# ScalarE in place of GpSimd for half of a 16-bit split ahead of a transposing DMA

## The chip, the cores and the metric

The kernel runs on 1 core of one Trainium2 chip. The metric is device time in microseconds, as a median of runs. Engine names follow the profile: PE is TensorE (matmul), PEld its weight loads, DVE VectorE, ACT ScalarE, POOL GpSimd, SP SyncE, which here only issues DMAs.

## What is computed

Two layers of a hybrid block over 256 tokens and 16 meta tokens (272 columns; the kernel keeps only the 258 it still needs towards the end of the second layer), width 1024. Each layer projects the normed input into retention, HGRN2 and differential attention, joins the three branches through gates, and ends in a convolutional feed-forward part. The change lies in differential attention, 8 heads per layer, each with two softmaxes:

```python
s = jnp.einsum('bqhmd,bkhmd->bhmqk', qb, k)
p = jax.nn.softmax(jnp.where(allowed, s, MASK_VALUE), axis=-1)
w = p[:, :, 0] - lam * p[:, :, 1]
return jnp.einsum('bhqk,bkhe->bqhe', w, v)
```

The weights `w` come out with queries on the partitions. The last product needs keys there, so `w` has to be transposed.

## The kernel before

**Main work.** Nearly all of PE's time goes to products of weights streamed from HBM, in 404 chunks of 8 tiles of 128x128. For each chunk, a DMA on SP's queue brings `wraw` (3 buffers), ACT copies it to `whi` (the rounded part), DVE subtracts to get `wlo` (the rest), each with 4 buffers. PE then makes three matmuls a tile: L943, L944 and L945. Chunk numbers stand in the names: `whi115` is the rounded half of chunk 115.

**Attention beside it.** `da_heads` (L1412 on) does two heads at a time: 2 layers x 2 groups x 2 pairs, so 8 pairs and 16 heads. PE makes the scores `ds`, DVE the masked maximum, ACT the exponentials, DVE the two scalings that leave `w` in the tile `two_a`. The second softmax's tile, `two_b`, is then free, and takes the 32-bit words of `w` parted into their upper and lower 16-bit halves, 3 blocks of 128 queries-by-keys words. A head does this in two instructions: ACT parts one block (L1463, 128x2x128 values), POOL the two others (L1464, 128x2x256 values). ACT also copies the block's short tail into `dt`. `turn` issues a DMA on SP's queue that transposes `two_b` back into `two_a`'s memory, and ACT copies the result, put together into words again, to `wts`. PE multiplies `wts` with the values `vt` into `do`, in one of two PSUM banks that accumulate (`acc_bank`). ACT copies two short pieces (`dot`) out of `do` and DVE the rest (`da`), and only then is the bank free for a later head. `da_tail` deals with a group's tails at once: `wt` is a transposition of `dt` on PE, DVE makes `tw` of it, and PE another `do` from `tw` and `vs`.

**Order.** The kernel is not written in the order in which it runs. Each operation goes into a plan with an estimated cost, and a list scheduler (`plan.issue`) writes the order of all engines and of SP's queue by these costs, the due times of the weights and the buffers that are free. A 16-bit copy that reads SBUF costs the planner 0.094 us + 1.163 ns a column on ACT, and 0.34 us + 0.85 ns a column on POOL. Once written, an engine's order is fixed: an instruction that waits holds up all behind it on its engine or queue. Since helpers record nearly every operation, the profile gives most instructions the line L634, and names tell them apart.

Of the kernel before, what the change touches and what calls it, by code (L numbers as in the profile page):

```python
# [15 lines left out]
AF = mybir.ActivationFunctionType  # L16
# [4 lines left out]
P = 128  # L21
# [671 lines left out]
def _trace(ctx, tc, plan, a, depth, probe):  # L693
    nc = tc.nc
    act = _Engine(plan, nc.scalar, "act", 0.094, 0.833e-3)
    dve = _Engine(plan, nc.vector, "dve", 0.068, 1.042e-3)
    pe = _Engine(plan, nc.tensor, "pe", 0.0, 4 / 2400)
    pool = _Engine(plan, nc.gpsimd, "pool", 0.04, 0.85e-3)
# [30 lines left out]
    def temp(cols, tag, bufs=2):  # L729
        return new(tp, [P, cols], F32, tag, bufs, tag)  # L730
# [7 lines left out]
    def acc_bank(name):  # L738
        return new(bp, [P, 512], F32, "acc", 2, name)

    def tt(out, x, y, op):
        dve.tensor_tensor(out=out, in0=x, in1=y, op=op)

    def stt(out, x, s, y, op0, op1):
        dve.scalar_tensor_tensor(out=out, in0=x, scalar=s, in1=y, op0=op0, op1=op1)

    def ts(out, x, s1, s2, op0, op1=ALU.bypass):
        dve.tensor_scalar(out=out, in0=x, scalar1=s1, scalar2=s2, op0=op0, op1=op1)
# [230 lines left out]
    def words(t):  # L979

        return t.bitcast(U16).rearrange("p (t h) -> p h t", h=2)

    def turn(to, src):

        turned = to.rearrange("p (n x) -> p n x", x=P)
        sync.dma_start_transpose(turned, src)
        return turned.rearrange("p (h n) x -> p h n x", h=2)
# [54 lines left out]
    for li in range(depth):  # L1042
# [370 lines left out]
        def da_heads(b, heads):  # L1413

            q, k, vt, out = st[f"dq{b}"], st[f"dk{b}"], st[f"dvt{b}"], st[f"da{b}"]
            scale = DA_DH ** -0.5

            a1s = [temp(T + P + TAIL, "wts") for _ in heads]
            tiles = ((META + P, T, 0), (META, META + P, T))
            sbs = [[temp(2 * T, tag) for tag in ("two_a", "two_b")] for _ in heads]  # L1420
            sss = [[new_bank("ds") for _ in range(2)] for new_bank in (bank, acc_bank)]
            stats = []
            for _ in heads:
                red = temp(12, "dm")
                stats.append([red[:, 4 * i : 4 * i + 4].rearrange("p (t m) -> p t m", m=2) for i in range(3)])


            def scores():
                for ss, hd in zip(sss, heads):
                    for q0, nk, at in tiles:  # L1430
                        for m in range(2):
                            half = slice(64 * m, 64 * m + 64)
                            nc.tensor.matmul(ss[m][:, at : at + nk], q[half, hd, q0 : q0 + P], k[half, hd, :nk], start=True, stop=True)  # L1433

            got = plan.add("pe", scores, 1.8, [x[:, : T + P + META] for ss in sss for x in ss], [q[:, heads[0] : heads[-1] + 1, :], k[:, heads[0] : heads[-1] + 1, :]], count=32)
            plan.hold(*sum(sbs, []), *a1s)
            for a1, hd in zip(a1s, heads):
                pool.tensor_copy(a1[:, :META], st[f"dw{b}"][:, hd * META : (hd + 1) * META])
                plan.queue(plan.ops[-1], got)
            for ss, sb, (nm, _, _) in zip(sss, sbs, stats):  # L1440
                for i, (q0, nk, at) in enumerate(tiles):
                    mask = const[:, C_MASK + T - nk : C_MASK + T]
                    for m in range(2):
                        cols = slice(at, at + nk)
                        dve.tensor_tensor_reduce(out=sb[m][:, cols], in0=ss[m][:, cols], in1=mask, scale=1.0,
                                                 scalar=-3e38, op0=ADD, op1=ALU.max, accum_out=nm[:, i, m : m + 1])
                ts(nm, nm, -scale, None, MUL)
            for sb, (nm, sm, cf) in zip(sbs, stats):
                for i, (q0, nk, at) in enumerate(tiles):
                    for m in range(2):  # L1450
                        p = sb[m][:, at : at + nk]
                        act.activation(p, p, AF.Exp, bias=nm[:, i, m : m + 1], scale=scale, accum_out=sm[:, i, m : m + 1])
                dve.reciprocal(cf, sm)
                tt(cf[:, :, 1], cf[:, :, 1], nlam[:, li : li + 1].to_broadcast([P, 2]), MUL)
                for i, (q0, nk, at) in enumerate(tiles):
                    p0, p1 = (x[:, at : at + nk] for x in sb)
                    ts(p1, p1, cf[:, i, 1:2], None, MUL)
                    stt(p0, p0, cf[:, i, 0:1], p1, MUL, ADD)
            for a1, sb, hd in zip(a1s, sbs, heads):
                w = sb[0]  # L1460
                src, to = (x[:, : 3 * P].bitcast(U16) for x in (sb[1], w))
                parts = src.rearrange("p (h t) -> p h t", h=2)
                act.activation(parts[:, :, :P], words(w[:, T : T + P]), AF.Copy)  # L1463
                pool.tensor_copy(parts[:, :, P:], words(w[:, : 2 * P]))  # L1464
                act.activation(st[f"dt{b}"][:, :, hd, :], tails_of(w), AF.Copy)
                turned = turn(to, src)
                act.activation(words(a1[:, META : META + 3 * P]), turned.rearrange("p h n x -> p h (n x)"), AF.Copy)
            for a1, hd in zip(a1s, heads):
                o = acc_bank("do")
                ec = slice(hd * P, hd * P + P)  # L1470
                pe.matmul(o[:, t0:T], vt[:, 0, ec], a1[:, t0:T], start=True, stop=False)
                pe.matmul(o[:, P + META : T], vt[:, 1, ec], a1[:, T : T + P], start=False, stop=True)
                for g, c in ((0, 2 * P), (1, P)):
                    act.activation(st[f"do{b}"][:, g, hd, :], o[:, c : c + TAIL], AF.Copy)
                dve.tensor_copy(out[:, hd, t0 : 2 * P], o[:, t0 : 2 * P])
                sub_norm(out[:, hd, t0 : 2 * P], out[:, hd, t0 : 2 * P])

        def tails_of(w):

            return bass.AP(w.tensor, w.offset + 2 * P, [list(w.ap[0]), [T - P, 2], [1, TAIL]])  # L1480

        def sub_norm(out, o):
            n = o.shape[1]
            r = temp(T, "hr")[:, :n]
            head_rsqrt(r, o, AF.Square)
            stt(out, o, subg[:, li : li + 1], r, MUL, MUL)
# [123 lines left out]
        for name, j in ORDER:  # L1610
            if name == "+ret":
                behind(ret_tail, "ret", 2)
                for hd in range(RET_HEADS):
                    behind(lambda: ret_head(hd), "ret", 2)
            elif name in ("+hga", "+hgb"):
                b = "ab".index(name[3])
                st[f"hgo{b}"] = behind(lambda: hg_heads(b), "hg" + name[3])
            elif name in ("+hgoa", "+hgob"):
                behind(st["hgo" + str("ab".index(name[4]))], "hgo" + name[4])
            elif name in ("+daa", "+dab"):  # L1620
                b = "ab".index(name[3])
                st[f"da{b}"] = slot4("da")
                behind(lambda: da_first(b), "da", 2)
                for hd in (0, 2):
                    behind(lambda: da_heads(b, (hd, hd + 1)), "da", 2)
                behind(lambda: da_tail(b), "da", 2)
            elif name[0] == "!":
                settle(name[1:])
            elif name[0] == "*":
                plan.key = clock[0] - MARGIN  # L1630
                n = name[1:]
                if n == "b2":
                    blocks = [st["da0"], st["da1"]]
                else:
                    t = st["rg" if n == "b0" else "hg"]
                    blocks = [t[:, 0:4, :], t[:, 4:8, :]]
                st["x" + n] = split_blocks(n, blocks, t0)
# [88 lines left out]
            elif name == "fi":  # L1726
# [16 lines left out]
                for f in range(2):  # L1743
                    ft = j + f * FK
                    w = lambda i: small[:, S_CW + (li * 3 + i) * 2 * FK + ft : S_CW + (li * 3 + i) * 2 * FK + ft + 1]
# [49 lines left out]
```

## Time and profile before

| | |
|---|---|
| median of 3 runs | 1279.19 us (1279.06 to 1281.21) |
| the profiled execution | 1278.5 us |
| its span in the trace | 1276.1 us |
| PE busy | 1267.3 us |
| DVE busy | 961.8 us |
| ACT busy | 871.5 us, 1481 instructions |
| POOL busy | 140.5 us, 125 instructions |

Busy time is the union of an engine's instructions in the trace. Some 2.4 us of the profiled execution lie around the span. The weights' stream feeds PE all the time, and the heads' chains run beside it on the other engines, so that a long busy time on these engines costs nothing by itself: time is lost where PE has nothing it may do next.

### The profile page before, as it was taken

How to read it: one execution, taken by the hardware profiler on the slowest of the kernel's cores; microseconds unless marked ns; L12 is line 12 of the kernel's file. 1: busy time of each engine (PE TensorE's matmuls, PEld its weight loads, DVE VectorE, ACT ScalarE, POOL GpSimd, SP SyncE). 2: the span in 40 equal slices, each digit the busy share in tenths (PEclk: the TensorE clock that was granted, in tenths of full speed). 3: DMA queues.
4: the chain of work that ended last, by engine and by line, in shares of the span. 5: the costliest groups of instructions: out<-in, count | busy, mean ns of one | idle time of the engine just before them, and what ended most of it. 6: DMA issues, size and time to landing. Idle time of an engine off the chain costs nothing.

```text
span 1276.1 us, 26835 instructions
## 1 busy us (share of the span) xinstructions
PE 1267.3 (99%) x10760; PEld 1246.5 (98%) x10760; DVE 961.8 (75%) x1690; ACT 871.5 (68%) x1481; POOL 140.5 (11%) x125
## 2 busy tenths in 40 slices
PE   9999999999999999999999999999999999999998
PEld 9999999999999999999999999999999999999986
DVE  8585887698785789886575858886987867998753
ACT  7776485857786577776456654858577865788743
POOL 1001101312232000000000011012232210000000
PEclk9999999999999999999999999999999999999999
DMA  7764685646656655556555656856556666677663
GB/s 235 246 184 133 191 219 139 164 150 166 190 154 187 189 173 179 172 178 182 173 177 180 182 166 176 219 152 166 157 154 199 183 197 187 181 197 205 202 191 106
DMA packets 102059, 229.19 MB, mean 180 GB/s; under 512 B 48176, under 2 KB 48304, under 8 KB 101936
## 3 DMA queue, kind: packets, MB, share of 16 engines
q1 hardware_dynamic: 101648, 226.97, 61.4%
q8 instruction: 84, 1.38, 0.4%
q10 hardware_dynamic: 288, 0.52, 0.1%
q14 instruction: 39, 0.32, 0.1%
HBM read 216.19 MB, written 1.05 MB: 170 GB/s over the span
## 4 chain that ended last, share of the span: by engine, by line
PE 95%; issue 2%; DVE 1%; POOL 1%; ACT 0%; DMA 0%; SPq 0%; ACTq 0%; POOLq 0%; DVEq 0%
PE main L945 29%; PE main L943 28%; PE main L944 28%; PE fo L1586 1%; PE fo L1584 1%; PE fo L1585 1%; PE ds L1433 1%; PE ro L634 1%; POOL hr L634 1%; PE do L634 1%; PE ho L1016 1%; PE lev L1152 1%; PE s L634 0%; PE px L1016 0%; PE far L1152 0%
## 5 line engine op out<-in xcount | busy, mean ns | idle before, releaser
L943 PE MATMUL main<-xh,whi 128*128 128x272 f32 (+1 forms) x2368 | 682.0, 288 | 0.1
L945 PE MATMUL main<-xh,wlo 128*128 128x272 f32 (+1 forms) x2368 | 679.8, 287 | 0.2 <-DVE wlo L634 0.2
L944 PE MATMUL main<-xl,whi 128*128 128x272 f32 (+1 forms) x2368 | 670.2, 283 | 0.0
L634 DVE TENSOR_TENSOR wlo<-wraw,whi 128x1024 fp32r<-128x1024 f32 (+1 forms) x408 | 499.4, 1228 | 217.3 <-ACT whi L634 215.8
L634 ACT ACTIVATE whi<-wraw 128x1024 fp32r<-128x1024 f32 (+1 forms) x408 | 426.8, 1048 | 185.3 <-PE main L944 124.3
L944 PEld LDWEIGHTS main<-xl,whi 128*128 128x128 f32 x2368 | 449.4, 190 | 0.0
L943 PEld LDWEIGHTS main<-xh,whi 128*128 128x128 f32 x2368 | 445.5, 188 | 1.2 <-ACT whi L634 0.4
L945 PEld LDWEIGHTS main<-xh,wlo 128*128 128x128 f32 x2368 | 444.5, 188 | 0.7 <-DVE wlo L634 0.6
L634 POOL PARTITION_ALL_REDUCE hr<-hsq x36 | 74.3, 2091 | 174.4 <-ACT hsq L634 159.0
L634 DVE SCALAR_TENSOR_TENSOR two_b<-u,small,two_b 128x256 f32<-128x256 f32 (+2 forms) x176 | 78.7, 492 | 0.2
L945 PE MATMUL main<-ghi,wlo 128*128 128x272 f32 x176 | 51.1, 290 | 0.0
L943 PE MATMUL main<-ghi,whi 128*128 128x272 f32 x176 | 50.8, 288 | 0.0
L944 PE MATMUL main<-glo,whi 128*128 128x272 f32 x176 | 50.2, 285 | 0.0
L634 ACT ACTIVATE two_b<-u,small 128x272 f32<-128x272 f32 (+1 forms) x88 | 49.1, 598 | 1.1 <-DVE glo L634 1.0
L634 POOL PARTITION_ALL_REDUCE rstd<-sum x4 | 10.5, 2614 | 326.5 <-PE main L944 193.5
L634 ACT ACTIVATE u<-main 128x544 f32<-128x544 f32 (+1 forms) x40 | 24.4, 610 | 28.2 <-PE main L945 28.1
L943 PE MATMUL main<-b0hi,whi 128*128 128x272 f32 (+1 forms) x128 | 37.4, 292 | 0.0
L943 PE MATMUL main<-b1hi,whi 128*128 128x272 f32 (+1 forms) x128 | 36.9, 288 | 0.0
L945 PE MATMUL main<-yhi,wlo 128*128 128x272 f32 (+1 forms) x128 | 36.5, 285 | 0.0
L945 PE MATMUL main<-b2hi,wlo 128*128 128x272 f32 (+1 forms) x128 | 36.5, 285 | 0.0
L945 PE MATMUL main<-b1hi,wlo 128*128 128x272 f32 (+1 forms) x128 | 36.5, 285 | 0.0
L945 PE MATMUL main<-b0hi,wlo 128*128 128x272 f32 (+1 forms) x128 | 36.5, 285 | 0.0
(256 smaller groups left out, 1940.8 us busy)
## 6 DMA issues: line engine op xcount, KB each, us to landing
wraw<-in_w SPq DMA_DIRECT2D x402, 512.0 KB, 3.7
h<-in_h SPq DMA_DIRECT2D x4, 272.0 KB, 4.8
dec<-in_dec SPq DMA_DIRECT2D x2, 544.0 KB, 5.4
wraw<-in_w SPq DMA_DIRECT2D x4, 256.0 KB, 4.4
const<-in_const SPq DMA_DIRECT2D x1, 937.0 KB, 8.4
gain<-in_gl SPq DMA_DIRECT2D x1, 512.0 KB, 4.5
out<-y ACTq DMA_DIRECT2D x2, 256.0 KB, 2.7
out<-y SPq DMA_DIRECT2D x2, 256.0 KB, 2.7
```

Of the source, the lines that this page charges most:

```text
L634: self.plan.add(self.name, lambda: f(*args, **kw), cost, outs, ins, self._kind(method, args, ins), count)
L943: nc.tensor.matmul(o, wh, hi, start=first, stop=False)
L944: nc.tensor.matmul(o, wh, lo, start=False, stop=False)
L945: nc.tensor.matmul(o, wl, hi, start=False, stop=last)
L1016: nc.tensor.matmul(o, x, y, start=first, stop=last)
L1152: nc.tensor.matmul(o, keys, x, start=True, stop=True)
L1433: nc.tensor.matmul(ss[m][:, at : at + nk], q[half, hd, q0 : q0 + P], k[half, hd, :nk], start=True, stop=True)
L1584: nc.tensor.matmul(o, gh, wh, start=first, stop=False)
L1585: nc.tensor.matmul(o, gl, wh, start=False, stop=False)
L1586: nc.tensor.matmul(o, gh, wl, start=False, stop=end)
```

## The change

One line: the two blocks that POOL parted are parted by ACT. The values written and where they go are the same.

```diff
@@ -1461,7 +1461,7 @@
                 src, to = (x[:, : 3 * P].bitcast(U16) for x in (sb[1], w))
                 parts = src.rearrange("p (h t) -> p h t", h=2)
                 act.activation(parts[:, :, :P], words(w[:, T : T + P]), AF.Copy)
-                pool.tensor_copy(parts[:, :, P:], words(w[:, : 2 * P]))
+                act.activation(parts[:, :, P:], words(w[:, : 2 * P]), AF.Copy)
                 act.activation(st[f"dt{b}"][:, :, hd, :], tails_of(w), AF.Copy)
                 turned = turn(to, src)
                 act.activation(words(a1[:, META : META + 3 * P]), turned.rearrange("p h n x -> p h (n x)"), AF.Copy)
```

It runs once per head, 16 times. The planner sees other costs and another engine, and so writes another order around each pair. POOL's other instructions keep their order.

The first place is the last pair of layer 1, whose heads have `two_a_337` and `two_a_339`. ACT's rows there before the change:

```order
L634 ACTIVATE whi114_800<-wraw114_799 128x4x256
L634 ACTIVATE two_b_340_691<-two_a_339_690 128x2x128
L634 ACTIVATE dt_315_666<-two_a_339_690 128x2x16
L634 ACTIVATE whi115_803<-wraw115_802 128x4x256
L634 ACTIVATE wts_335_686<-two_a_337_688 128x2x384
L634 ACTIVATE wts_336_687<-two_a_339_690 128x2x384
L634 ACTIVATE whi116_807<-wraw116_806 128x4x256
L634 ACTIVATE dot_316_667<-do_347_698 128x16
L634 ACTIVATE hsq_349_700<-da_310_661 128x256
L634 ACTIVATE dot_316_667<-do_347_698 128x16
L634 ACTIVATE m2_380_797<-main_379_790 128x544
L634 ACTIVATE whi117_810<-wraw117_809 128x4x256
```

The same place on ACT after the change:

```order
L634 ACTIVATE two_b_338_689<-two_a_337_688 128x2x256
L634 ACTIVATE whi115_803<-wraw115_802 128x4x256
L634 ACTIVATE two_b_340_691<-two_a_339_690 128x2x128
L634 ACTIVATE dt_315_666<-two_a_339_690 128x2x16
L634 ACTIVATE two_b_340_691<-two_a_339_690 128x2x256
L634 ACTIVATE whi116_807<-wraw116_806 128x4x256
L634 ACTIVATE wts_335_686<-two_a_337_688 128x2x384
L634 ACTIVATE m2_380_797<-main_379_790 128x544
L634 ACTIVATE wts_336_687<-two_a_339_690 128x2x384
L634 ACTIVATE whi117_810<-wraw117_809 128x4x256
L634 ACTIVATE dot_316_667<-do_347_698 128x16
L634 ACTIVATE hsq_349_700<-da_310_661 128x256
```

The second head's parting now stands behind `whi115`, both `wts` behind `whi116`, and the `dot` copies of `do_347_698`, whose PSUM bank the head after next needs, behind `whi117`.

On SP's queue, which issues the DMAs, the same place before the change:

```order
L634 DMA wraw115_802<-in_w 128x1024
L634 DMA_TRANSPOSE two_a_337_688<-two_b_338_689 128x6x128
L634 DMA_TRANSPOSE two_a_339_690<-two_b_340_691 128x6x128
L634 DMA wraw116_806<-in_w 128x1024
L634 DMA wraw117_809<-in_w 128x1024
```

And after it:

```order
L634 DMA wraw115_802<-in_w 128x1024
L634 DMA wraw116_806<-in_w 128x1024
L634 DMA_TRANSPOSE two_a_337_688<-two_b_338_689 128x6x128
L634 DMA_TRANSPOSE two_a_339_690<-two_b_340_691 128x6x128
L634 DMA wraw117_809<-in_w 128x1024
```

The load of chunk 116 is issued ahead of the two transposing DMAs instead of behind them. On PE, the two heads' products of this pair (`do_347_698` and `do_350_701`) stand one chunk, 8 tiles, later; `wt_353_704` also stands 8 tiles later and the tails' product 10. The other products of the 8 pairs stay where they were or move by 1 to 9 tiles (in layer 2's last pair by 6 to 9).

The second place is the second pair of layer 1's first group (`two_a_261` and `two_a_263`). ACT's rows before:

```order
L634 ACTIVATE vsrc_303_648<-main_300_639 128x512
L634 ACTIVATE whi93_715<-wraw93_714 128x4x256
L634 ACTIVATE whi94_720<-wraw94_719 128x4x256
L634 ACTIVATE two_b_264_567<-two_a_263_566 128x2x128
L634 ACTIVATE dt_239_542<-two_a_263_566 128x2x16
L634 ACTIVATE tails_302_647<-main_305_650 128x32 x2
L634 ACTIVATE vsrc_306_657<-main_305_650 128x512 x2
L634 ACTIVATE whi95_723<-wraw95_722 128x4x256
L634 ACTIVATE vt_301_646<-vtr_304_649 128x2x256 x2
L634 ACTIVATE wts_259_562<-two_a_261_564 128x2x384
```

And after (`vsrc`, `tails` and `vt` belong to the next group's values):

```order
L634 ACTIVATE two_b_262_565<-two_a_261_564 128x2x256
L634 ACTIVATE whi93_715<-wraw93_714 128x4x256
L634 ACTIVATE two_b_264_567<-two_a_263_566 128x2x128
L634 ACTIVATE dt_239_542<-two_a_263_566 128x2x16
L634 ACTIVATE tails_302_647<-main_305_650 128x32
L634 ACTIVATE two_b_264_567<-two_a_263_566 128x2x256
L634 ACTIVATE tails_302_647<-main_305_650 128x32
L634 ACTIVATE vsrc_306_657<-main_305_650 128x512 x2
L634 ACTIVATE whi94_720<-wraw94_719 128x4x256
L634 ACTIVATE vt_301_646<-vtr_304_649 128x2x256
L634 ACTIVATE whi95_723<-wraw95_722 128x4x256
L634 ACTIVATE wts_259_562<-two_a_261_564 128x2x384
```

Two 128x2x256 partings now stand ahead of `wts_259_562`, and one of the two `vt` copies has moved behind it. The product on PE that reads `wts_259_562` (`do_271_574`) keeps its place among the tiles.

## The prediction

> **What bounds the kernel now.** I read the page's busy times first, then what PE waited for, then the one wait that the change touches, back along the engines. The first row of the page:
>
> ```profile
> PE 1267.3 (99%) x10760; PEld 1246.5 (98%) x10760; DVE 961.8 (75%) x1690; ACT 871.5 (68%) x1481; POOL 140.5 (11%) x125
> ```
>
> PE is busy for 1267.3 of 1276.1 us. Nothing on POOL, ACT or DVE can save more than the 8.8 us that PE is idle, and most of these lie at the start and the end of the span. Where PE waits, by the view of its waits (what it waited for: us in total, times, longest), as far as the layers' middle is concerned:
>
> ```profile
> PE wt L634 <- DVE wts L634: 1.0, 1, 1.0
> ...
> PE do L634 <- issue: 0.7, 1, 0.7
> PE main L945 <- DVE wlo L634: 0.2, 1, 0.2
> ```
>
> In the whole of both attentions PE stands still twice: the `wt` row (layer 2's first pair starts there, and the order of that place isn't touched by the change) and the `do` row. The `do` wait lies in the pair whose order the change rewrites most, layer 1's last. PE's timeline there (start, length, idle before):
>
> ```profile
> 386.97 0.28 PE L944 MATMUL main<-xl,whi 128*128 128x272 f32 x1
> 387.09 0.29 PE L945 MATMUL main<-xh,wlo 128*128 128x272 f32 x1
> ...
> 388.09 0.92 PE L634 MATMUL do<-wts,vt 128*128 128x272 f32 x4 [0.71 <-issue]
> ```
>
> Matmuls start 0.12 us apart, so the next was due at 387.21 and came at 388.09: a stall of **0.88 us** (the view counts 0.71, since it lets the last matmul end later). It is named "issue", so no releaser was seen. The instruction is the pair's second product, `do_350_701`. It needs one of two PSUM banks; one is held by the first product, `do_347_698`, until ACT's two `dot` copies have left it. ACT at the same time:
>
> ```profile
> 383.98 1.07 ACT L634 ACTIVATE wts<-two_a 128x768 uint16<-128x768 uint16 x1 [1.12 <-DMA two_a<-two_b]
> ...
> 386.49 1.06 ACT L634 ACTIVATE whi<-wraw 128x1024 fp32r<-128x1024 f32 x1 [1.45 <-DMA wraw<-in_w]
> 387.45 0.17 ACT L634 ACTIVATE dot<-do 128x16 f32<-128x16 f32 x1
> 387.51 0.41 ACT L634 ACTIVATE hsq<-da 128x256 f32<-128x256 f32 x1
> 387.82 0.17 ACT L634 ACTIVATE dot<-do 128x16 f32<-128x16 f32 x1
> ```
>
> The second `dot` ends at 387.99, and PE goes on 0.10 later. The `dot` copies stand behind `whi116`, and this one waited 1.45 us for a weight load. That load was late because SP's queue stood behind a transposing DMA:
>
> ```profile
> 376.68 0.33 SPq L634 DMA_DIRECT2D wraw<-in_w  x1
> 377.11 5.33 SPq L634 DMA_TRANSPOSE two_a<-two_b  x2
> 382.52 1.48 SPq L634 DMA_DIRECT2D wraw<-in_w  x3
> ```
>
> Two transposes hold the queue from 377.11 to 382.44, and what the second waits for is POOL's copy, first row below. The second row is the same copy for another pair, and behind them stand the subtractions that DVE made beside each:
>
> ```profile
> 377.93 3.26 POOL L634 COPY two_b<-two_a 128x512 uint16<-128x512 uint16 x1 [2.45 <-DVE two_a L634]
> ```
>
> ```profile
> 312.90 0.61 POOL L634 COPY two_b<-two_a 128x512 uint16<-128x512 uint16 x1 [1.78 <-DVE two_a L634]
> ```
>
> ```profile
> 378.36 2.36 DVE L634 TENSOR_TENSOR wlo<-wraw,whi 128x1024 fp32r<-128x1024 f32 x2
> ```
>
> ```profile
> 312.97 2.75 DVE L634 TENSOR_TENSOR wlo<-wraw,whi 128x1024 fp32r<-128x1024 f32 x2 [0.19 <-ACT whi L634]
> ```
>
> The copy took 3.26 us in place of 0.61 and ended at 381.19, 0.47 after the two subtractions beside it. So the chain of the 0.88 us is: POOL's copy stretched beside DVE, second transpose late, load of chunk 116 late, `whi116` late, `dot` late, PSUM bank late. The other direction shows in pair two of layer 1: the copy began first (312.90, and 312.97 for DVE) and was not stretched, but the two subtractions took 2.75 instead of 2.36, 0.39 more. The Trainium skill, "SBUF — State Buffer", section "Who interferes with whom", has a rule for both: a DVE instruction with two SBUF inputs and a GpSimd instruction that reads SBUF exclude each other, and the one that started first keeps the other out. By that rule, the trace agrees: 3.26 where DVE was under way, and 0.39 lost by DVE where POOL was first.
>
> **What an instruction costs on its new engine.** Groups by line and form, ACT first, then POOL (count | busy us, mean ns | idle before):
>
> ```profile
> L634 ACT ACTIVATE whi<-wraw 128x1024 fp32r<-128x1024 f32 x400 | 422.0, 1057 | 183.3 <-PE main L944 122.4 <-PE fo L1585 26.0 <-DMA wraw<-in_w 19.4
> L634 ACT ACTIVATE vsrc<-main 128x512 uint16<-128x512 uint16 x48 | 26.8, 597 | 0.0
> L634 ACT ACTIVATE vt<-vtr 128x512 uint16<-128x512 uint16 x32 | 25.2, 794 | 1.8 <-DMA vtr<-vsrc 1.8
> ...
> L634 ACT ACTIVATE two_b<-two_a 128x256 uint16<-128x256 uint16 x16 | 6.5, 408 | 2.3 <-DVE two_a L634 2.3
> ```
>
> ```profile
> L634 POOL COPY two_b<-two_a 128x512 uint16<-128x512 uint16 x16 | 20.0, 1250 | 71.7 <-DVE two_a L634 46.0 <-issue 25.7
> ```
>
> ACT at 128x512 for this copy isn't in the trace. The bounds are 0.597 (`vsrc`, the same width out of PSUM) and 0.794 (`vt`, the same width from a transposed tile). The same kind at 256 takes 0.408 and `whi` at 1024 takes 1.057, so 0.845 ns a column, and 0.408 + 256 x 0.845 ns = **0.62 us**. I take that: `two_b` is the nearest row. ACT gets 16 x 0.62 = 9.9 us, and POOL loses 20.0. Where it falls (busy us by stage, layer 1's attention, then layer 2's):
>
> ```profile
> core 0: us, PE busy (x) PEld busy (x) DVE busy (x) ACT busy (x) POOL busy (x), PEclk, DMA share, GB/s
> 278.00:396.00 118.00, 117.29 (x937) 114.74 (x936) 91.87 (x208) 88.67 (x198) 34.62 (x28) 1.00 0.63 175
> 918.00:1030.00 112.00, 112.00 (x930) 109.86 (x929) 88.96 (x207) 89.04 (x198) 34.15 (x31) 1.00 0.64 183
> ```
>
> ACT is busy for 177.7 of 230 us there, and would be for 187.6, which is 82%. It isn't the bound, and what hides the 9.9 us is ACT's own idle time ahead of `whi`: 183.3 us in the kernel, 122.4 of it waiting for PE to leave a buffer. The sum therefore takes the copies at nothing, **as long as each single chain keeps its spare time**. Two places decide that.
>
> **Place one, layer 1's last pair.** Its products come 8 tiles later in the new order. PE's rows of the pair now, of which the first starts chunk 112 and the second is `do_347_698`:
>
> ```profile
> 379.47 0.27 PE L634 MATMUL wt<-const,dt 128*128 128x128 f32 x1
> ...
> 384.29 0.84 PE L634 MATMUL do<-wts,vt 128*128 128x272 f32 x4
> ```
>
> A tile is three matmuls of 0.12 us, 0.373 more exactly, so 8 tiles are 2.98 us: `do_347_698` moves to 387.3, and `do_350_701`, due at 387.2 without its stall, to 390.2. Now the chain before it. `whi115` needs the buffer that PE leaves as chunk 112 starts, 379.5, and is done at 380.6. Then come the second head's small parting (0.41), `dt` (about 0.2) and the new copy (0.62): 381.8 at worst, where POOL's copy ended at 381.19. The second transpose goes out some 0.6 later than now, to 383.1. The load of chunk 116 no longer waits for it, as it stands ahead of both transposes. The load of chunk 117 does: issued at 383.1, landed 3.7 to 4.4 later (386.49 − 382.52 = 4.0 for `wraw` above), at 387.1, `whi117` done at 388.2, then `dot`, `hsq`, `dot` by 388.9 as the rows at 387.45 to 387.99 space them. The bank is free at 389.0, and due at 390.2. **The 0.88 us goes**, with 1.2 us to spare. What is late next here is `wts`: the two follow `whi116`, and transposes that land at 386.2 at the latest let the first end at 387.2, just where PE wants it (387.3). That is the thinner margin of the two; the landing times decide:
>
> ```profile
> DMA to landing us min/median/max: 2.5/3.1/4.4
> ```
>
> 386.2 is the first head's transpose issued by 381.8 and landed after the maximum of 4.4; the median of 3.1 leaves 1.3 us.
>
> **Place two, layer 1's second pair.** Two of the new copies and no later product. ACT, and the PE row that reads the first `wts`:
>
> ```profile
> 316.26 1.43 ACT L634 ACTIVATE vt<-vtr 128x512 uint16<-128x512 uint16 x2
> 317.53 1.08 ACT L634 ACTIVATE wts<-two_a 128x768 uint16<-128x768 uint16 x1
> ```
>
> ```profile
> 319.59 0.84 PE L634 MATMUL do<-wts,vt 128*128 128x272 f32 x4
> ```
>
> `wts` ends at 318.61 and has 0.98 us to spare. The order puts 2 x 0.62 ahead of it and takes one `vt` away (two took 317.53 − 316.26 = 1.27, so 0.64): 0.60 later, with 0.38 left. No stall. The weights of chunk 93 wait behind one new copy, 0.62, and get back the 0.39 that DVE lost to POOL there.
>
> **The other pairs.** The first head's spare in the first and in the last pair:
>
> ```profile
> 291.02 1.09 ACT L634 ACTIVATE wts<-two_a 128x768 uint16<-128x768 uint16 x1 [1.10 <-DMA two_a<-two_b]
> ```
>
> ```profile
> 295.05 0.84 PE L634 MATMUL do<-wts,vt 128*128 128x272 f32 x4
> ```
>
> ```profile
> 1019.62 1.09 ACT L634 ACTIVATE wts<-two_a 128x768 uint16<-128x768 uint16 x1
> ```
>
> ```profile
> 1022.13 0.82 PE L634 MATMUL do<-wts,vt 128*128 128x258 f32 x4
> ```
>
> 295.05 − 292.11 = 2.94 and 1022.13 − 1020.71 = 1.42. In the last pair the products also move 6 tiles later (2.1 us). With 0.62 more, neither stalls, and between these the planner's moves of 1 to 5 tiles go with the chains. I take them at nothing.
>
> **Sum.** 1278.5 for the profiled execution − 0.88 = 1277.6. The median of the runs, 1279.19, is 0.7 above that execution, so **1278.3 us** against it, 0.07% less. About 0.2%, 2.6 us, is what a measurement of this kernel can tell from no change.
>
> **Rivals.**
> - *The stall comes back elsewhere.* Place one's margin for `wts` is gone if a transpose lands at its slowest, and the `dot` copies now wait behind `whi117` as they did behind `whi116`. For it: the same queueing of ACT behind a weight load made the stall of now. Against it: products 2.98 us later. At the same price of about 0.9 the time is 1279.2.
> - *Slower: ACT's row is late in each pair.* The new copy delays the parting's end, hence the transpose, hence `wts`, and PE waits at `do`. With a slow landing (4.4 for 3.1: 1.3) and the copy (0.62), 1.92 in all, the three spares above leave 0.94, 0.50 and 0: 0.48 as their mean, over 8 pairs 3.8 us. It decides from the point where median landing exceeds some 4 us. For it: the slowest landing is in the trace. Against it: POOL's copies took 1.25 us on average by the group above, so that on ACT the parting is the shorter one in most pairs. 1278.5 + 3.8 − 0.9 + 0.7 = 1282.1.
> - *Faster: DVE gets its time back.* 16 copies on POOL that hold DVE up by 0.39 at most make 6.2 us. On PE's path only the waits on DVE count, 1.0 (`wt`) and 0.2 (`wlo`). Against it: neither lies beside a copy of POOL. 1278.3 − 1.2 = 1277.1. The rule of the Trainium skill named above leads here, since without GpSimd's reads DVE's subtractions would find the way free at all times.
>
> **Chances.** Forecast 0.52, stall elsewhere 0.21, slower 0.20, faster 0.07. The range reaches from the faster case, with the 0.39 of one more copy (1276.7), to the slower one with two copies at their upper bound (0.17 more each, 1282.4). Slower by over 0.2% is over 1281.7: most of the slower case, 0.18. Faster by over 0.2% is under 1276.6, which the faster case reaches only with more than one copy's time on top: 0.04 of its 0.07. The rest, 0.78, is within.
>
> **What would show it.** Right: POOL's groups without `two_b`; ACT's `two_b<-two_a 128x512` at about 0.62; no wait of PE at the `do` of layer 1's last pair; PE's busy time as now. The second transpose of that pair would be issued near 383, and `whi117` would run before PE gets to `do`. Wrong: new rows of PE waiting for ACT `wts` or for "issue" at a `do`; transposes that land beyond 4 us; `whi` or `wlo` late in chunks 93 and 94; or a copy on ACT well over 0.8, since the bounds come from other tiles.

## The result and the profile after

The changed kernel takes **1278.12 us** (median of 19 runs, 1277.27 to 1279.12). The kernel before, run 19 times beside it, took 1281.19 us (1279.06 to 1284.67), so the ratio is 0.9977, with a 95% interval of 0.9970 to 0.9984: faster by 3.07 us, 0.23%. In three later comparisons the kernel before had medians of 1279.68, 1279.75 and 1279.56 us (33, 33 and 30 runs); kernels with the new order gain 1.3 to 1.6 us on those; the changed kernel itself was not run in them again. What differs between the two kernels is not the median alone: single runs of before reach up to 1285 us, while those of after lie within 2 us.

The page and the view of PE's waits, after:

```profile
PE 1267.8 (99%) x10760; PEld 1246.8 (98%) x10760; DVE 961.2 (75%) x1690; ACT 878.2 (69%) x1497; POOL 116.3 (9%) x109
```

```profile
PE wt L634 <- DVE wts L634: 1.0, 1, 1.0
...
PE ds L634 <- ACT wts L634: 0.4, 1, 0.4
PE main L945 <- DVE wlo L634: 0.3, 1, 0.3
```

ACT has 16 instructions more and POOL 16 fewer. The wait at `do` is gone, and a new one stands at a `ds` in layer 2. In the groups by form, the new copy, and the small one for comparison:

```profile
L634 ACT ACTIVATE two_b<-two_a 128x512 uint16<-128x512 uint16 x16 | 9.9, 618 | 0.0
...
L634 ACT ACTIVATE two_b<-two_a 128x256 uint16<-128x256 uint16 x16 | 6.5, 406 | 2.3 <-DVE two_a L634 2.2
```

Place one, layer 1's last pair: PE (`wt`, then the two heads' products), ACT, and SP's queue.

```profile
383.08 0.27 PE L634 MATMUL wt<-const,dt 128*128 128x128 f32 x1
...
387.90 0.84 PE L634 MATMUL do<-wts,vt 128*128 128x272 f32 x4
```

```profile
390.82 0.84 PE L634 MATMUL do<-wts,vt 128*128 128x272 f32 x4
```

```profile
381.56 0.61 ACT L634 ACTIVATE two_b<-two_a 128x512 uint16<-128x512 uint16 x1
383.22 1.06 ACT L634 ACTIVATE whi<-wraw 128x1024 fp32r<-128x1024 f32 x1 [1.05 <-PE main L944]
385.72 1.08 ACT L634 ACTIVATE wts<-two_a 128x768 uint16<-128x768 uint16 x1 [1.44 <-DMA two_a<-two_b]
...
388.13 1.06 ACT L634 ACTIVATE whi<-wraw 128x1024 fp32r<-128x1024 f32 x1
...
389.62 0.17 ACT L634 ACTIVATE dot<-do 128x16 f32<-128x16 f32 x1
```

```profile
379.31 0.33 SPq L634 DMA_DIRECT2D wraw<-in_w  x1
380.15 3.26 SPq L634 DMA_TRANSPOSE two_a<-two_b  x2
383.50 2.39 SPq L634 DMA_DIRECT2D wraw<-in_w  x3
```

Chunk 116's load is issued alone at 379.31, ahead of the transposes, and `whi116` (383.22) waits for PE's buffer, no longer for that load. The second `dot` ends at 389.79 and the second product starts at 390.82, directly behind the matmul before it: 1.03 us to spare where 0.88 were lost.

The span is 0.4 us longer all the same, because two other things differ between these two executions. The first scores of layer 1 and then of layer 2, before and after:

```profile
278.75 1.68 PE L1433 MATMUL ds<-dk,dq 64*128 64x272 f32 x16
```

```profile
918.12 1.68 PE L1433 MATMUL ds<-dk,dq 64*128 64x272 f32 x16
```

```profile
279.35 1.68 PE L1433 MATMUL ds<-dk,dq 64*128 64x272 f32 x16
```

```profile
917.88 1.68 PE L1433 MATMUL ds<-dk,dq 64*128 64x272 f32 x16
```

After was already 0.60 us behind when the first attention began, where the two programs have the same order, and 0.24 ahead at layer 2: it gained 0.84 between, about the stall of 0.88. Then the new wait at `ds` took 0.4 to 0.6 of it back. One execution of each can't show a difference of 0.2%; the medians can.

### The profile page after: what moved, and what is told of

It is laid out like the page before. It is cut to its first block, busy times and chain, and to the rows that moved or that the text cites. A ratio compares the mean times of both kernels' runs of the same rounds, so it can differ in the third digit from the quotient of the medians.

```text
span 1276.5 us, 26830 instructions
## 1 busy us (share of the span) xinstructions
PE 1267.8 (99%) x10760; PEld 1246.8 (98%) x10760; DVE 961.2 (75%) x1690; ACT 878.2 (69%) x1497; POOL 116.3 (9%) x109
## 4 chain that ended last, share of the span: by engine, by line
PE 92%; issue 2%; ACT 2%; DVE 1%; POOL 1%; DMA 1%; SPq 0%; DVEq 0%; POOLq 0%; ACTq 0%
PE main L945 28%; PE main L943 28%; PE main L944 27%; PE fo L1586 1%; PE fo L1584 1%; PE fo L1585 1%; PE ds L1433 1%; PE ro L634 1%; POOL hr L634 1%; PE do L634 1%; PE ho L1016 1%; PE lev L1152 1%; PE s L634 0%; ACT whi L634 0%; DMA wraw<-in_w 0%
```

## Experiments

All times are medians; "before" is the kernel before in the same comparison.

| kernel | us (range) | before | ratio, 95% interval |
|---|---|---|---|
| before_again | 1279.47 (1278.74 to 1281.01) | 1279.68 | 0.9999 (0.9990 to 1.0008) |
| old_order_act | 1280.18 (1279.30 to 1281.07) | 1279.68 | 1.0001 (0.9992 to 1.0009) |
| new_order_pool | 1278.15 (1277.29 to 1278.55) | 1279.68 | 0.9983 (0.9974 to 0.9992) |
| new_plus_pool | 1278.37 (1277.61 to 1278.69) | 1279.68 | 0.9985 (0.9976 to 0.9993) |
| pair4_act | 1278.29 (1277.34 to 1279.32) | 1279.75 | 0.9987 (0.9978 to 0.9995) |
| others_act | 1283.48 (1281.21 to 1286.14) | 1279.75 | 1.0030 (1.0020 to 1.0040) |
| pair4_pool_twice | 1281.28 (1280.33 to 1284.41) | 1279.75 | 1.0012 (1.0001 to 1.0022) |
| cost_pool | 1277.92 (1277.51 to 1278.99) | 1279.75 | 0.9985 (0.9976 to 0.9993) |
| load_first | 1279.51 (1278.92 to 1282.26) | 1279.56 | 1.0000 (0.9992 to 1.0009) |
| products_later | 1279.86 (1279.18 to 1284.75) | 1279.56 | 1.0004 (0.9995 to 1.0014) |
| new_order_pool_twice | 1277.92 (1277.18 to 1278.48) | 1279.56 | 0.9980 (0.9971 to 0.9989) |
| after_visits_later | 1276.68 (1276.37 to 1276.93) | 1279.56 | 0.9972 (0.9961 to 0.9983) |

### The engine or the order?

Two kernels part what one line of the change joined: the engine that runs the copies, and the order that the planner writes for it. `run` is what an operation of the plan issues; replacing it leaves the order alone.

**before_again**, no edit.

> The kernel before, unchanged, once more, to get a second profile of it. If all of the gain is the one PE stall of the first profile (0.88 us in layer 1's last pair), this profile shows that stall again, between 0.5 and 1.3 us, and no other one over 0.3 us in the attention. If the rest of the gain of 3.07 us is POOL's copies that DVE stretches differently from run to run, this profile shows other copies stretched (over 1 us), PE waits of 1.5 to 4 us in sum behind them, and single times spread over 1279 to 1285.

**old_order_act**, the order of before with copies on ACT:

```diff
                 pool.tensor_copy(parts[:, :, P:], words(w[:, : 2 * P]))
+                plan.ops[-1].run = lambda o=parts[:, :, P:], i=words(w[:, : 2 * P]): nc.scalar.activation(o, i, AF.Copy)
```

> The order of before, kept as it is, with the 16 copies run by ACT at the place where POOL's were issued. Theory 1 (what counts is that POOL's copy is stretched by DVE): nearly all of the gain stays, 1278 to 1279, spread under 2 us, no PE wait at the `do` of layer 1's last pair. Theory 2 (the planner's new order brings the gain, products 8 tiles later): the gain is gone, 1280.5 to 1282.5.

**new_order_pool**, the order of after with copies on POOL:

```diff
                 act.activation(parts[:, :, P:], words(w[:, : 2 * P]), AF.Copy)
+                plan.ops[-1].run = lambda o=parts[:, :, P:], i=words(w[:, : 2 * P]): nc.gpsimd.tensor_copy(o, i)
```

> The order of after, kept as it is, with the 16 copies run by POOL. Theory 1 (the stretched copy): slower than after, 1280 to 1284, with a spread of several us, as the order counts on 0.6 us and POOL takes up to 3.3. Theory 2 (the order): as after, 1278 to 1279.

**new_plus_pool**, after with 16 idle copies on POOL:

```diff
     fixed([P, KD], "pad")
+    idle_copy = fixed([P, 2 * P], "idle_copy").bitcast(U16).rearrange("p (h t) -> p h t", h=2)
...
                 act.activation(parts[:, :, P:], words(w[:, : 2 * P]), AF.Copy)
+                both = plan.ops[-1]
+                both.run = lambda f=both.run, i=parts[:, :, P:]: (f(), nc.gpsimd.tensor_copy(idle_copy, i))
```

> After, with 16 copies on POOL added that read what ACT's copy has just written and that nobody waits for (their result isn't used): POOL's reads beside DVE are back, without any wait on POOL. Theory 1a (POOL's copy harms by being late itself, as a link of the chain): as after, 1277.8 to 1278.6. Theory 1b (POOL's reads harm by keeping DVE out, 0.39 us each): PE waits for DVE's `wlo` or `tw`, 1279 to 1282.

The second profile of before shows the same single stall in the attention, 0.8 by this view:

```profile
PE do L634 <- issue: 0.8, 1, 0.8
```

With the new order, POOL does as well as ACT. Some of its copies are still stretched (shortest, median and longest in ns), but at layer 1's last pair they took 1.56 and 0.61 us, where before had 0.61 and 3.26:

```profile
L1465 POOL COPY two_b<-two_a x16: 614/616/2683, 286.3 to 1016.5; 128x512 uint16<-128x512 uint16 x16
```

```profile
378.61 1.56 POOL L1465 COPY two_b<-two_a 128x512 uint16<-128x512 uint16 x1 [8.76 <-issue]
381.34 0.61 POOL L1465 COPY two_b<-two_a 128x512 uint16<-128x512 uint16 x1 [1.17 <-DVE two_a L634]
```

So the new order by itself also ends the long stretch at the place of the stall, and this run alone doesn't settle theory 1 there; new_order_pool_twice below does, with long copies in the new order.

In the old order, ACT as the engine in all pairs gains nothing: 1280.18 us, between the ranges of the two theories. Its profile has lost layer 1's stall, but PE waits in three places of layer 2 instead, at products and at the tails' `do`:

```profile
961.36 0.89 PE L634 MATMUL do<-wts,vt 128*128 128x258 f32 x4 [0.74 <-issue]
```

```profile
1019.19 0.49 PE L634 MATMUL do<-tw,vs 128*128 128x128 f32 x2 [0.23 <-DVE tw L634]
1021.40 0.78 PE L634 MATMUL do<-wts,vt 128*128 128x258 f32 x3 [0.65 <-ACT wts L634]
```

The idle copies of new_plus_pool cost nothing that can be measured: 0.22 us more than new_order_pool, well within either range. So POOL's reads beside DVE do no harm to the time by themselves, and theory 1b falls.

### One place, or the pairs together?

The same edit as in old_order_act, under a condition.

**pair4_act**: ACT for layer 1's last pair alone. **others_act**: ACT for all but that pair.

```diff
                 pool.tensor_copy(parts[:, :, P:], words(w[:, : 2 * P]))
+                if (li, b, heads[0]) == (0, 1, 2):     # others_act: if not (...)
+                    plan.ops[-1].run = lambda o=parts[:, :, P:], i=words(w[:, : 2 * P]): nc.scalar.activation(o, i, AF.Copy)
```

> The order of before, with ACT in place of POOL for the two heads of layer 1's last pair alone (the place of the 0.88 us stall); the other 14 copies stay on POOL. If that stall and what hangs on it is all that parts before from after: no PE wait at that `do`, none new in layer 2, 1278.0 to 1278.6, all runs under 1279.5. If the difference is spread over the pairs: 1279 to 1280 and single runs over 1281 as before.

> The other half: the order of before, ACT for the 14 copies of the other pairs, POOL for layer 1's last pair. If the copies on ACT cost what they cost in the old order's layer 2 (waits of 0.9, 0.4 and 0.8 us there): the sum of the stall of 0.9 and these 2.1, so slower than before by 1 to 2.5 us, 1280.5 to 1282.5, with single runs over 1282. If ACT's copies were free in any order: as before, 1279.2 to 1280.

One pair is nearly all of it: pair4_act gains 1.46 us, where kernels with the new order gain 1.3 to 1.6. There the chain of the prediction runs as it was drawn, with its first link mended (SP, ACT, then PE's second product):

```profile
377.66 3.04 SPq L634 DMA_TRANSPOSE two_a<-two_b  x2
380.79 10.44 SPq L634 DMA_DIRECT2D wraw<-in_w  x5
```

```profile
378.85 0.61 ACT L1466 ACTIVATE two_b<-two_a 128x512 uint16<-128x512 uint16 x1
...
384.67 1.06 ACT L634 ACTIVATE whi<-wraw 128x1024 fp32r<-128x1024 f32 x1 [0.33 <-DMA wraw<-in_w]
...
386.58 0.17 ACT L634 ACTIVATE dot<-do 128x16 f32<-128x16 f32 x1
```

```profile
387.78 0.84 PE L634 MATMUL do<-wts,vt 128*128 128x272 f32 x4
```

The transposes leave the queue after 3.04 us in place of 5.33, the load goes out at 380.79 in place of 382.52 although this profile runs 0.6 us late, and the second `dot` is done 1.03 us ahead of the product. others_act costs 3.7 us, more than the 1 to 2.5 that were expected. In its profile (1282.18 us, 1.3 under its median) two waits for "issue" sum to 3.2, one of 2.3 at place one and one in layer 2.

```profile
PE do L634 <- issue: 3.2, 2, 2.3
```

At place one that kernel has the instructions and the order of before, and POOL's second copy is as long (3.32 us for 3.26); still PE waits 2.3 in place of 0.7. The load of chunk 116, first of three issued in a row, and `whi116`:

```profile
383.05 1.48 SPq L634 DMA_DIRECT2D wraw<-in_w  x3
```

```profile
388.56 1.06 ACT L634 ACTIVATE whi<-wraw 128x1024 fp32r<-128x1024 f32 x1 [2.99 <-DMA wraw<-in_w]
```

5.5 us lie between, where the profiles of before had 4.0 (382.52 to 386.49) and 4.1. That is where these profiles differ: three loads of 512 KB are issued in 1.5 us, and the first of them, for which all wait, comes early in one and late in another. Why isn't shown. Nor is it shown that before itself ever gets to 2.3: others_act differs from it in the other pairs, and all of its 11 runs lie over 1281.2 us. In the new order that load is not faster but earlier. It goes out alone, and in new_order_pool `whi116` starts 4.2 us after it (379.72 to 383.94), waiting for it; in after, `whi116` starts 3.9 us behind the load, but waits for PE's buffer by then.

### Longer copies, and TensorE's clock

**pair4_pool_twice**, before with POOL's copies of that pair made twice; **new_order_pool_twice**, new_order_pool with the copies of that pair made twice.

```diff
                 pool.tensor_copy(parts[:, :, P:], words(w[:, : 2 * P]))
+                if (li, b, heads[0]) == (0, 1, 2):
+                    plan.ops[-1].run = lambda o=parts[:, :, P:], i=words(w[:, : 2 * P]): [nc.gpsimd.tensor_copy(o, i) for _ in range(2)]
```

> Before, with POOL's copies of layer 1's last pair made twice each, so that the stall there gets longer. If a copy's lateness goes into PE's wait in full: the wait grows from 0.9 by 0.6 (one copy) to 3 us, 1280.3 to 1283. If long waits also bring down TensorE's clock (the slowest run of before has a mean clock of 0.997 against 0.999 for most), the trace shows slices of a lower clock behind the wait and the time grows by more than the wait. If the copy's lateness is hidden by something else: as before.

> The new order, all copies on POOL, and those of layer 1's last pair made twice, as in the run that made the old order lose 1.5 us and stand still for 2.2. If the new order has the 1.2 us to spare at that product that the prediction worked out, and no load behind the transposes: 1278.0 to 1279.2, a PE wait of at most 0.8 there, no slice of a lower clock. If the new order only happens to fit the usual lengths: 1280 to 1283.

Old order: the median grows by 1.5 us. The profile fell on the second slowest of 10 runs (1283.14): PE's stall is 2.35 us there (388.60 to 390.95), and then its matmuls are further apart. Windows across it (PE, PEld, DVE, ACT, POOL busy, then the granted clock):

```profile
388.48 0.29 PE L945 MATMUL main<-xh,wlo 128*128 128x272 f32 x1
390.95 1.35 PE L634 MATMUL do<-wts,vt 128*128 128x272 f32 x4 [2.18 <-issue]
...
394.14 0.43 PE L943 MATMUL main<-xh,whi 128*128 128x272 f32 x1
394.37 0.43 PE L944 MATMUL main<-xl,whi 128*128 128x272 f32 x1
...
395.02 0.29 PE L945 MATMUL main<-xh,wlo 128*128 128x272 f32 x1
```

```profile
388.00:392.00 4.00, 1.82 (x12) 1.47 (x10) 1.22 (x1) 3.55 (x7) 1.13 (x1) 0.91 0.62 250
392.00:396.00 4.00, 4.00 (x24) 4.00 (x24) 2.90 (x4) 2.30 (x8) 3.06 (x2) 0.66 0.48 140
396.00:400.00 4.00, 4.00 (x34) 4.00 (x33) 1.88 (x3) 3.36 (x7) 1.63 (x4) 1.00 0.54 182
```

0.23 us from matmul to matmul in place of 0.12, until about 394.7: 24 matmuls in a window that holds 34, so some 1.2 us more are lost there, 10 x 0.12. The stall of others_act, no shorter (2.3 by the view that says 2.18 here), was followed by a full clock:

```profile
392.00:396.00 4.00, 4.00 (x34) 4.00 (x33) 3.35 (x4) 2.95 (x7) 3.06 (x3) 1.00 0.68 228
```

So a stall of this length was followed by a lower clock in one profile and not in the other.

New order: nothing of this, 1277.92 us. POOL took 2.2 us for each head of that pair:

```profile
378.35 2.24 POOL L1465 COPY two_b<-two_a 128x512 uint16<-128x512 uint16 x2 [8.76 <-issue]
381.43 2.18 POOL L1465 COPY two_b<-two_a 128x512 uint16<-128x512 uint16 x2 [0.84 <-DVE two_a L634]
```

PE has no wait at `do`, though the second copy ends 1.7 us later than in the profile of before (383.61 for 381.19, less the 0.75 by which this profile runs late); the second `dot` is done 0.43 us ahead of its product. So the room that the new order leaves takes in 1.6 us more of copies for a head, and a long copy on POOL is no harm there.

### The planner's estimate

**cost_pool**, before with POOL's copies, and only the planner's idea of their cost raised:

```diff
             elif self.name == "pool" and method == "tensor_copy":
-                cost += 0.3
+                cost += 0.3 + (0.94e-3 * n if ins[0].dtype == U16 else 0.0)
```

> Before, with POOL's copies still on POOL, and only the planner's estimate of their cost raised from 0.78 to 1.26 us (the trace's mean is 1.25). The planner then puts the last pair's products 6 to 7 tiles later. If the place of the products decides: no stall in that pair, 1277.9 to 1278.7, as after. If copies on ACT are needed: as before, 1279.2 to 1280.

1277.92: as good as the changed kernel, with every copy still on POOL. The estimate, 0.78 us where the trace's mean is 1.25, is enough to explain why the old order left no room.

### Which part of the order?

The rest takes single rows of the finished order and puts them elsewhere. An operation's new place moves those that depend on it, if they would come too early; nothing else.

```diff
-        order = [None] + self.order()
+        order = _moved(self, [None] + self.order())
```

**load_first**, in the order of before:

```python
    load = next(o for o in at if o.engine == "sp" and has(o, "wraw116"))
    turn = min((o for o in at if o.func == "turn" and has(o, "two_b_338")), key=at.get)
    return [(load, at[turn] - 0.5)]
```

> Before, with one row moved: on SP's queue the load of chunk 116 is issued ahead of the two transposing DMAs of layer 1's last pair (where the changed kernel has it). PE, ACT, DVE and POOL keep their order, and POOL makes the copies. If the chain of the stall runs through that load (copy late, second transpose late, load late, `whi116` late, `dot` late): `whi116` starts near 385 instead of 386.5, the stall goes, 1278.0 to 1278.8. If the `dot` copies are late for another reason: the stall stays, 1279.2 to 1280.

The stall moved instead of going. The load had to wait for its buffer until 380.81, when DVE's subtraction of an earlier chunk had ended (380.79), so that both transposes went out behind it (SP), `wts` came late (ACT), and PE waits for it at the pair's first product:

```profile
381.23 2.55 SPq L634 DMA_TRANSPOSE two_a<-two_b  x2
```

```profile
385.57 1.97 ACT L634 ACTIVATE wts<-two_a 128x768 uint16<-128x768 uint16 x2 [3.12 <-DMA two_a<-two_b]
```

```profile
386.77 0.92 PE L634 MATMUL do<-wts,vt 128*128 128x272 f32 x4 [1.12 <-ACT wts L634]
```

**products_later**, in the order of before:

```python
    out = []
    for name in ("do_347", "do_350"):
        for o in at:
            if o.engine == "pe" and has(o, name):
                behind = [m for m in tiles if at[m] > at[o]]
                out.append((o, at[behind[3]] + 0.1))
    return out
```

> Before, with one thing moved on PE: the products of layer 1's last pair stand 4 tiles (1.5 us) later; ACT, POOL and SP's queue keep their order. If the place of the products decides, the 0.88 us are absorbed whatever makes the `dot` copies late: 1278.0 to 1278.8, and of the longer stalls of single executions (2.3 us was seen) under 1 us stays. If the products' place only moves the wait: 1279.2 to 1280.

No gain here either. The profile fell on one of the slowest of its runs (1283.30, two of 12 over 1281), with a stall of 3.9 us. SP's loads, ACT, DVE and PE's second product:

```profile
382.86 2.45 SPq L634 DMA_DIRECT2D wraw<-in_w  x3
```

```profile
389.66 1.06 ACT L634 ACTIVATE whi<-wraw 128x1024 fp32r<-128x1024 f32 x1 [2.60 <-DMA wraw<-in_w]
392.34 0.18 ACT L634 ACTIVATE dot<-do 128x16 f32<-128x16 f32 x1 [1.63 <-DVE da L634]
```

```profile
390.75 1.23 DVE L634 TENSOR_TENSOR wlo<-wraw,whi 128x1024 fp32r<-128x1024 f32 x1 [6.96 <-ACT whi L634]
391.89 0.42 DVE L634 COPY da<-do 128x256 f32<-128x256 f32 x1
```

```profile
393.00 1.20 PE L634 MATMUL do<-wts,vt 128*128 128x272 f32 x4 [3.79 <-ACT dot L634]
```

6.8 us passed from the load's issue to `whi116` in this execution, and the second transpose was late too: ACT's second `wts` waited 2.81 us for it, where in the profile of before 1.12. And moving the product later moved DVE's `da` behind `wlo116`, which waits for `whi116`; the bank is held by `da` too. So later products alone only queue the bank's release behind more of the same late chunk, and this edit isn't a pure test of the place on PE. What helps is likely both: a load that goes ahead of the transposes, and products late enough for transposes that go behind it. Taken singly, each shifts the wait; the planner's new order has the two, but the old order with just these two moves was not run.

### A faster kernel

PE's remaining waits in after are of one kind with the one that went: an instruction stands in PE's order a little ahead of what it needs. **after_visits_later** moves two of them.

```python
    out = []
    for name, step in (("wt_682", 3), ("ds_757", 1)):
        for o in at:
            if o.engine == "pe" and has(o, name) and not o.func == "x" and any(n.startswith("wts_") for n in o.tiles):
                behind = [m for m in tiles if at[m] > at[o]]
                out.append((o, at[behind[step]] + 0.1))
    return out
```

> After, with the two instructions of PE in layer 2 that it still waits at moved on: `wt` (1.2 us, it waits for DVE's `wts`) stands 4 tiles later, and the `ds` that reads ACT's `wts` (0.6 in the profile of after, 0.2 in another) 2 tiles later; the other engines keep their order. If later places absorb these waits as they did in layer 1: 1276.5 to 1277.3. If what hangs on them is late in turn (the scores behind them): 1277.8 to 1278.6.

1276.68 us (6 runs), 1.24 below new_order_pool_twice on the same chip, and the smallest range of all. PE's waits at both are gone; `wt` now starts directly behind the matmul before it:

```profile
915.27 0.33 PE L634 MATMUL wt<-const,wts 128*128 128x64 f32 x2
```

## Why the prediction was right in direction and small in size

**Right: place one.** The pair's stall goes, and the chain came out nearly as worked out. This profile runs 0.6 us late there (279.35 against 278.75). Less that, the second new copy ends at 381.6 (381.8 was said), the transposes leave at 382.8 (383.1), the second `dot` ends at 389.2 (388.9), and the second product starts at 390.2 (390.2), with 1.03 us to spare for 1.2. `do_347_698` stands at 387.3, as said. One sign of being wrong did show, a transpose that landed after 5.6 us (median 3.2), but PE waits at no `do` of the pairs.

**Right: the copy's price and its cover.** 0.618 us for 0.62, 9.9 in sum, and no pair in the new order waits for it. At place two the working was too pessimistic: the first `wts` ends 0.1 us later than before, not 0.60 (319.29 for 318.61, less the 0.6), and PE comes to it 0.9 later. But the cover belongs to the new order. In the old one it is gone: old_order_act loses in layer 2 what it wins in layer 1, and others_act is 3.7 us slower. The slower rival had a part of this (`wts` late behind the copies: one of old_order_act's three new waits, 0.65); the longest, 0.74 for "issue", has `dot` copies behind a `whi` that waited 0.98 for its load, as at place one. And the rival decides where the prediction didn't look for its condition: not by how fast transposes land, but by whether the planner knows of the copies.

**Right, but not the only way: POOL's stretched copy as the root.** When that copy started, at 377.93, DVE was in this subtraction, ahead of the two that the prediction shows:

```profile
377.73 0.72 DVE L634 TENSOR_TENSOR y<-y,m 128x544 f32<-128x544 f32 x1
```

pair4_act shows that ending the stretch at that one pair is enough. new_order_pool_twice shows that in the new order a long copy does no harm. The prediction told the two as one cause; they are two remedies for one wait, and the change has both.

**Wrong in size: the stall as "0.88", and 1279.19 as what the kernel takes.** The step that puts the median 0.7 above the profiled execution took three runs and one profile for a kernel whose runs scatter over 6 us. The profiled execution of before, 1278.5, is below all of the 19 runs compared with it. Over 19 runs the median was 2.7 above it, and 1.1 to 1.3 in the three later comparisons. By the view of PE's waits the same product waited 0.7, 0.8 and 2.3 us in three profiles that have before's rows at that place (before, before_again and others_act), by when the load of chunk 116 landed. The 0.88 (0.7 by the view) was the short end. So the gain was 1.3 to 3.1 us in place of 0.9, and 0.23% fell just over the bound of 0.2%, for which the prediction had a chance of 0.04. That the time itself, 1278.3, came within 0.2 us of the measured 1278.12 is in part luck: the 0.7 was added to a kernel whose median lies 0.2 below its profiled execution (1278.35), and the wait at `ds`, which the sum doesn't have, makes up for a part of it.

**Missed: `ds` in layer 2.** The planner's small moves were taken at nothing. One place made a wait of 0.4 to 0.6 us, 0.2 in new_order_pool: of two `wts` copies that ACT made one behind the other before, the second now stands behind a `whi`, and `ds` waits for it. Moving the `ds` took the wait away.

**Fallen: the faster rival.** DVE's busy time fell by 0.6 us (961.8 to 961.2), far from 16 x 0.39, and none of it was on PE's path: new_plus_pool gives POOL's reads back to no measurable effect.

**Open.** In the three later comparisons the gain is about 1.5 us, and the stall in the two profiles of before is 0.9 and 1.0, counted as in the prediction. Where the rest lies within a typical run is not placed, since the first 20 us alone differ by more than that from execution to execution. That late loads and the clock behind long stalls make the slow single runs of before fits the runs' clocks (of 33 runs in one comparison, seven lie over 1281 us, four of these at a mean clock of 0.998 or less; of the other 26, one does), but no profile of the kernel before itself fell on such a run.

## What to carry to other kernels

When a planner writes the order, an edit to one instruction's engine is an edit to the order of everything near it: run the old order with the new engine and the new order with the old engine before you credit either, and look in each at the place of the wait, since an order can shorten the same copy too. A measured mean in place of a guessed cost (1.25 us for 0.78) can be worth as much as moving the work. And where a kernel's single runs scatter, one profile and three runs may give the floor and not the price of a wait: look for what lets the same wait come out at 0.7 us in one profile and at 2.3 in another.

## What the runs showed of the hardware

Three 512 KB loads issued within 1.5 to 2.5 us of each other land at very different times: from the first one's issue to the copy that waits for it 4.0 (before), 4.1 (before_again), 4.8 (pair4_pool_twice), 5.5 (others_act) and 6.8 us (products_later). One that went ahead of the transposes took 4.2 (new_order_pool), so the load that went alone was not faster there. After a PE stall of 2.35 us the granted clock averaged 0.66 over a window of 4 us, and matmuls were at their usual distance again some 3.8 us after PE had resumed; after the 3.9 us of products_later it averaged 0.69 over such a window; after a stall of 2.4 us in others_act it did not fall. The Trainium skill, "TensorE: Matmul & The Clock Gate", Part 1, puts the fall to half clock down to one idle window of about 3.4 us that runs freely. The matmuls' spacing, 0.23 us for 0.12, agrees with a half clock, and a free-running window would fit the difference between the stalls of 2.35 and 2.4 us; but a stall of 2.35 us was enough here, so less than a full idle window did it.
